# Weight gradient: narrow G of slice 0 alone in 1 KB rows, slice 1's G whole by the software queue, and a finer first rounding

## Chip, cores, metric

One core of one Trainium2 chip. Time is device microseconds of one launch; fast runs of the kernel before agree within 0.35 us in each set, so a change of less than 0.2 us is read from profiles, not from a few times. Instruction times count from the span's start; the span is about 1.8 us shorter than the time of the launch. A transfer has landed when its completion semaphore has its full count. TensorE starts at half clock: the trace records when it goes to full clock, and the spacing of 512-column matmuls shows it too (0.43 us apart before, 0.216 after).

## The reference

`grad_weight[k, n] = sum over b, m of input[b, m, k] * grad_output[b, m, n]`, with 16 x 512 rows, K = 1024, N = 768, all fp32. Called X and G below: the 8192 rows are 64 slices of 128.

## The kernel before

X and G are rounded to bf16 on their way. From slice 2 on, the software queue (GpSimd) casts while it loads. Slices 0 and 1 come mostly by the hardware queues of SyncE and ScalarE as fp32 and are rounded by VectorE (DVE) and ScalarE (ACT), so that TensorE (PE) can start early. Each slice needs 12 matmuls of 512 columns: eight "wide" ones (blocks A and B; G columns 0 to 511 against eight blocks of X), and four "narrow" ones (N; G columns 512 to 767, two turned blocks, against two halves of X). PE first runs warm-up matmuls on constants.

```python
ORDER = "A1! B1 N1 B2! N2 A2 N3! A3 B3 A4! ...".split()      # cut; "B2!" = block B up to slice 1, then close its banks
WARMUP = [512] * 10 + [128] * 2

xf = [head.tile([P, K], f32, name=f"xf{s}") for s in range(2)]
gf = head.tile([P, NA], f32, name="gf")                      # NA = 512
gnf = head.tile([P, 2, NB], f32, name="gnf")                 # NB = 256
nc.sync.dma_start(out=gf, in_=G[0:P, 0:NA])
nc.scalar.dma_start(out=xf[0], in_=X[0:P, :])
nc.sync.dma_start(out=gnf, in_=G[0 : 2 * P, NA:N].rearrange("(s p) n -> p s n", p=P))
nc.scalar.dma_start(out=xf[1], in_=X[P : 2 * P, :])
# ... warm-up matmuls
gwide[1] = head.tile([P, NA], bf16, name="g1")
nc.gpsimd.dma_start(out=gwide[1], in_=G[P : 2 * P, 0:NA])
for s in range(2, S):                                        # gt, then xt, of each slice on the software queue
    ...

def add_slice(part, i, s, first, last):                      # cut
    ...
    if part.first:
        copy_out(dst, bank, i)                               # even i on DVE, odd i on ScalarE
        if s == 0 and i == 0:
            round_narrow(0)                                  # DVE: narrow G of slice 0, behind the copy of bank 0
```

## Time and profile before

| | before |
|---|---|
| time, median (range) | 176.97 us (176.78 to 176.98; the 3 runs known at the prediction) |
| PE busy | 169.8 of 175.0 us, 97% |
| first real matmul | 5.37 us |
| first narrow matmul | 7.82 us, though PE could go on at 7.11 |
| block B of slice 1 | 8.84 us; from there on PE never waits |

PE's busy share alone says "nothing to gain". The chain of waits and the timeline of the first 9 us, shown in the prediction, say where some 0.9 us of avoidable waiting lies: at the head, before and among the first four narrow matmuls.

### The profile page before, as it was taken

To read this page: it belongs to the slowest core of one execution; us is meant where nothing else is said; L and a number is where in the kernel's file an instruction comes from. 1 tells how busy PE (TensorE), PEld (TensorE's weight loads), DVE (VectorE), ACT (ScalarE), POOL (GpSimd) and SP (SyncE) were. 2 spreads that over 40 slices of the span, in tenths; PEclk is the share of its full clock that TensorE was granted. 3 is DMA by queue.
4 is the path that set the end of the run, shared out by engine and by line. 5 is a ranking of instruction groups with operands and counts; after the bars stand their busy time and mean duration, and the time that the engine had idled before them with its cause. 6 is when DMAs were issued, how large, how long until landed. Compare 5 with 4: busy or idle time off the path is not lost.

```text
span 175.0 us, 2012 instructions
## 1 busy us (share of the span) xinstructions
PE 169.8 (97%) x793; PEld 78.2 (45%) x808; DVE 61.5 (35%) x103; ACT 6.3 (4%) x12; POOL 66.4 (38%) x129
## 2 busy tenths in 40 slices
PE   8799999999999999999999999999999999999993
PEld 3244444444444444444444444444444444444463
DVE  0665574791950029400000561300460003932122
ACT  2640000000000000000000000000000000000000
POOL 7444443444444444444444444444174200000000
PEclk9999999999999999999999999999999999999999
DMA  5999999999999999999999999999999990085623
GB/s 189 290 207 208 209 208 207 208 208 209 209 207 207 209 208 209 208 209 207 208 208 208 208 211 206 208 208 209 209 207 209 208 184 3 0 182 161 167 93 120
DMA packets 25176, 33.42 MB, mean 191 GB/s; under 512 B 6480, under 2 KB 16720, under 8 KB 25168
## 3 DMA queue, kind: packets, MB, share of 16 engines
q0 software_dynamic: 18000, 28.58, 89.3%
q1 hardware_dynamic: 2720, 2.62, 4.6%
q10 hardware_dynamic: 4448, 2.10, 4.6%
q8 instruction: 6, 0.10, 0.2%
q14 instruction: 2, 0.02, 0.0%
HBM read 58.72 MB, written 3.15 MB: 353 GB/s over the span
## 4 chain that ended last, share of the span: by engine, by line
PE 93%; DMA 4%; issue 1%; DVE 0%; SPq 0%
PE bank L126 62%; PE bank L133 32%; DMA gnf<-in_grad_output_dram 4%; SPq L74 0%; DVE gn L114 0%; DVE acc L117 0%
## 5 line engine op out<-in xcount | busy, mean ns | idle before, releaser
L126 PE MATMUL bank<-gt,xt 128*128 128x512 bf16 (+2 forms) x515 | 108.3, 367 | 0.5
L126 PEld LDWEIGHTS <-xt 128*128 128x128 bf16 x524 | 50.2, 98 | 57.3
L117 DVE TENSOR_TENSOR acc<-bank,acc 128x512 f32<-128x512 f32 (+2 forms) x62 | 37.9, 666 | 73.4 <-PE bank L126 73.0
L133 PE MATMUL bank<-xt,gt 128*128 128x512 bf16 x242 | 54.8, 379 | 0.3
L98 POOL DMA_DIRECT2D xt<-in_input_dram x62 | 32.9, 531 | 37.7 <-DMA xt<-in_input_dram 35.2
L97 POOL DMA_DIRECT2D gt<-in_grad_output_dram x62 | 32.9, 531 | 31.9 <-DMA gt<-in_grad_output_dram 28.0
L133 PEld LDWEIGHTS <-gt 128*128 128x128 bf16 x248 | 24.3, 98 | 29.3
L117 DVE TENSOR_TENSOR acct<-bank,acct 128x512 f32<-128x512 f32 x24 | 15.7, 682 | 30.0 <-PE bank L133 29.9
L83 PE MATMUL bank<-const-bfloat16-1.0 128*128 128x512 bf16 (+1 forms) x12 | 4.3, 534 | 0.8 <-PEq L263 0.8
L126 PE MATMUL bank<-g,x 128*128 128x512 bf16 x16 | 4.0, 380 | 0.3 <-DVE x L110 0.3
L83 PEld LDWEIGHTS <-const-bfloat16-1.0 128*128 128x128 bf16 x12 | 1.5, 135 | 3.3 <-issue 3.2
L179 DVE STREAM_TRANSPOSE turned<-acct 128x512 f32<-128x512 f32 x4 | 2.9, 714 | 0.1
L121 DVE COPY acc<-bank 128x512 f32<-128x512 f32 x4 | 2.7, 686 | 0.6 <-PE bank L126 0.6
L133 PE MATMUL bank<-x,gn 128*128 128x512 bf16 x8 | 2.2, 380 | 0.5 <-DVE gn L114 0.5
L126 PEld LDWEIGHTS <-x 128*128 128x128 bf16 x16 | 1.5, 97 | 2.2 <-DVE x L110 0.5
L123 ACT COPY acc<-bank 128x512 f32<-128x512 f32 x4 | 2.1, 589 | 1.8 <-PE bank L126 1.8
L110 DVE CAST g<-gf 128x256 bf16<-128x256 f32 x1 | 0.3, 295 | 4.7 <-DMA gf<-in_grad_output_dram 4.7
L121 DVE COPY acct<-bank 128x512 f32<-128x512 f32 x2 | 1.3, 684 | 1.3 <-PE bank L133 1.3
L133 PEld LDWEIGHTS <-gn 128*128 128x128 bf16 x8 | 0.7, 98 | 1.9 <-DVE gn L114 1.0
L111 ACT CAST x<-xf 128x256 bf16<-128x256 f32 x4 | 1.4, 402 | 0.2 <-DMA xf<-in_input_dram 0.2
L111 ACT ACT_TABLE_LOAD x1 | 1.3, 1283 | 1.7 <-PEq L263 1.7
L123 ACT COPY acct<-bank 128x512 f32<-128x512 f32 x2 | 1.1, 589 | 1.5 <-PE bank L133 1.5
(8 smaller groups left out, 3.0 us busy)
## 6 DMA issues: line engine op xcount, KB each, us to landing
xt<-in_input_dram POOLq DMA_DIRECT2D x62, 256.0 KB, 8.5
gt<-in_grad_output_dram POOLq DMA_DIRECT2D x62, 192.0 KB, 8.5
out_dram<-acc SPq DMA_DIRECT2D x13, 128.0 KB, 2.7
xf<-in_input_dram ACTq DMA_DIRECT2D x2, 512.0 KB, 5.2
out_dram<-turned ACTq DMA_DIRECT2D x4, 256.0 KB, 3.4
gf<-in_grad_output_dram SPq DMA_DIRECT2D x1, 256.0 KB, 3.9
gnf<-in_grad_output_dram SPq DMA_DIRECT2D x1, 256.0 KB, 6.3
out_dram<-acc SPq DMA_DIRECT2D x1, 256.0 KB, 2.0
```

The lines of the kernel that those rows point to most:

```text
L83: nc.tensor.matmul(wps[:, 0:cols], ones, nc.const_aps.tensor(1.0, (P, cols), bf16), start=True, stop=True,)
L97: nc.gpsimd.dma_start(out=gt, in_=G[s * P : (s + 1) * P, :])
L98: nc.gpsimd.dma_start(out=xt, in_=X[s * P : (s + 1) * P, :])
L110: nc.vector.tensor_copy(out=dst[:, c : c + QX], in_=src[:, c : c + QX])
L111: nc.scalar.copy(out=dst[:, c + QX : c + 2 * QX], in_=src[:, c + QX : c + 2 * QX])
L117: nc.vector.tensor_add(out=dst, in0=src, in1=dst)
L121: nc.vector.tensor_copy(out=dst, in_=src)
L123: nc.scalar.copy(out=dst, in_=src)
L126: nc.tensor.matmul(bank, xs[s][:, k * P : (k + 1) * P], gwide[s][:, c0:c1], start=start, stop=stop)
L133: nc.tensor.matmul(bank, gnarrow[s].rearrange("p (r t) -> p t r", t=NT)[:, t], xs[s][:, h * NA : (h + 1) * NA], start=start, stop=stop,)
L179: nc.vector.transpose(out=turned[:, h * hb : (h + 1) * hb, :, t], in_=dst.rearrange("p (b r) -> p b r", r=SQ),)
```

## The change

The intent: narrow G of slice 0 should not have to share its transfer with slice 1's narrow G, whose rows take turns with X of slice 1. Slice 1's G goes whole to the software queue, which casts it, so DVE's cast of slice 1's narrow G falls away. DVE's first cast of X is cut to 128 columns, so that the first matmul starts sooner.

```diff
-    gf = head.tile([P, NA], f32, name="gf")
-    gnf = head.tile([P, 2, NB], f32, name="gnf")
-    nc.sync.dma_start(out=gf, in_=G[0:P, 0:NA])
+    gf = head.tile([P, N], f32, name="gf")
+    nc.sync.dma_start(out=gf[:, 0:NA], in_=G[0:P, 0:NA])
     nc.scalar.dma_start(out=xf[0], in_=X[0:P, :])
-    nc.sync.dma_start(out=gnf, in_=G[0 : 2 * P, NA:N].rearrange("(s p) n -> p s n", p=P))
+    nc.sync.dma_start(out=gf[:, NA:N], in_=G[0:P, NA:N])
     nc.scalar.dma_start(out=xf[1], in_=X[P : 2 * P, :])
...
-    nc.gpsimd.dma_start(out=gwide[1], in_=G[P : 2 * P, 0:NA])
-    for s in range(2, S):
+    for s in range(1, S):
         gt = xg.tile([P, N], bf16, name="gt")
         nc.gpsimd.dma_start(out=gt, in_=G[s * P : (s + 1) * P, :])
...
+    round_by("DVE", g0, gf, 0, 256)
+    round_by("ACT", g0, gf, 256, NA)
+    round_by("DVE", xs[0], xf[0], 0, P)
+    round_by("ACT", xs[0], xf[0], 2 * P, 4 * P)
+    round_by("DVE", xs[0], xf[0], P, 2 * P)
+    round_by("DVE", xs[0], xf[0], 4 * P, 6 * P)
+    round_by("ACT", xs[0], xf[0], 6 * P, 8 * P)
...
             if s == 0 and i == 0:
-                round_narrow(0)
+                round_by("DVE", g0, gf, NA, N)
```

More of the change, by code (lines that the diff above doesn't have):

```diff
@@ L89, with round_by @@
         )
-    gwide[1] = head.tile([P, NA], bf16, name="g1")
-    nc.gpsimd.dma_start(out=gwide[1], in_=G[P : 2 * P, 0:NA])
-    for s in range(2, S):
+    for s in range(1, S):
         gt = xg.tile([P, N], bf16, name="gt")
-        xt = xg.tile([P, K], bf16, name="xt")
         nc.gpsimd.dma_start(out=gt, in_=G[s * P : (s + 1) * P, :])
-        nc.gpsimd.dma_start(out=xt, in_=X[s * P : (s + 1) * P, :])
-        xs[s] = xt
         gwide[s] = gt[:, 0:NA]
         gnarrow[s] = gt[:, NA:N]
-    QX = 256
-    gwide[0] = head.tile([P, NA], bf16, name="g0")
+        if s > 1:
+            xs[s] = xg.tile([P, K], bf16, name="xt")
+            nc.gpsimd.dma_start(out=xs[s], in_=X[s * P : (s + 1) * P, :])
     for s in range(2):
         xs[s] = head.tile([P, K], bf16, name=f"x{s}")
-        gnarrow[s] = head.tile([P, NB], bf16, name=f"gn{s}")
-    def round_pair(dst, src, c):
-        nc.vector.tensor_copy(out=dst[:, c : c + QX], in_=src[:, c : c + QX])
-        nc.scalar.copy(out=dst[:, c + QX : c + 2 * QX], in_=src[:, c + QX : c + 2 * QX])
-    def round_narrow(s):
-        nc.vector.tensor_copy(out=gnarrow[s], in_=gnf[:, s, :])
+    g0 = head.tile([P, N], bf16, name="g0")
+    gwide[0] = g0[:, 0:NA]
+    gnarrow[0] = g0[:, NA:N]
+    def round_by(engine, dst, src, c0, c1):
+        copy = nc.vector.tensor_copy if engine == "DVE" else nc.scalar.copy
+        copy(out=dst[:, c0:c1], in_=src[:, c0:c1])
+    round_by("DVE", g0, gf, 0, 256)
[5 more added lines that the diff above has]
+    round_by("ACT", xs[0], xf[0], 6 * P, 8 * P)
     def add_out(dst, src):
@@ L209, in bank_by_bank @@
                 add_slice(part, i, s, s == first, s == upto - 1)
-    round_pair(gwide[0], gf, 0)
-    round_pair(xs[0], xf[0], 0)
-    round_pair(xs[0], xf[0], NA)
     for i, step in enumerate(ORDER):
         if i == 2:
-            round_pair(xs[1], xf[1], NA)
-            round_pair(xs[1], xf[1], 0)
-            round_narrow(1)
+            round_by("DVE", xs[1], xf[1], 4 * P, 6 * P)
+            round_by("ACT", xs[1], xf[1], 6 * P, 8 * P)
+            round_by("DVE", xs[1], xf[1], 0, 2 * P)
+            round_by("ACT", xs[1], xf[1], 2 * P, 4 * P)
         close = step.endswith("!")
```

## The prediction

> **What bounds the kernel now.** I read the page's busy shares first, then the chain that ended last, then the same chain in order of time, then the timeline of the first 12 us, and at last the trace's records of single instructions, DMA packets and landings for that stretch.
>
> Page, busy shares and chain:
>
> ```profile
> PE 169.8 (97%) x793; PEld 78.2 (45%) x808; DVE 61.5 (35%) x103; ACT 6.3 (4%) x12; POOL 66.4 (38%) x129
> ...
> PE 93%; DMA 4%; issue 1%; DVE 0%; SPq 0%
> PE bank L126 62%; PE bank L133 32%; DMA gnf<-in_grad_output_dram 4%; SPq L74 0%; DVE gn L114 0%; DVE acc L117 0%
> ```
>
> The matmuls are the bound, and only one thing besides them is on the chain: the transfer of narrow G into gnf. In order of time (start us, us, what):
>
> ```profile
> 1.18 6.27 DMA gnf<-in_grad_output_dram
> 7.45 0.02 issue
> 7.47 0.30 DVE gn L114
> 7.77 0.05 issue
> 7.82 1.19 PE bank L133 x4
> 9.01 0.86 PE bank L126 x4
> 9.87 0.86 PE bank L133 x4
> ```
>
> From 7.82 us to the last matmul the chain never leaves PE except for 0.05 us pieces of issue. So the end can be moved only by moving the step at 7.8 us, and whatever is gained there is gained at the end, provided that no later wait appears. The timeline shows who waits around it:
>
> ```profile
> 5.37 1.90 PE L126 MATMUL bank<-g,x 128*128 128x512 bf16 x8 [0.33 <-DVE x L110]
> 5.80 0.69 DVE L121 COPY acc<-bank 128x512 f32<-128x512 f32 x1 [0.28 <-PE bank L126]
> ...
> 7.47 0.29 DVE L114 CAST gn<-gnf 128x256 bf16<-128x256 f32 x1 [0.98 <-DMA gnf<-in_grad_output_dram]
> 7.68 0.68 DVE L121 COPY acc<-bank 128x512 f32<-128x512 f32 x1
> ...
> 7.82 1.19 PE L133 MATMUL bank<-x,gn 128*128 128x512 bf16 x4 [0.55 <-DVE gn L114]
> ...
> 8.84 1.02 PE L126 MATMUL bank<-g,x 128*128 128x512 bf16 x4
> ```
>
> A steady matmul of 512 columns takes 0.216 us from start to start. The eighth matmul of slice 0's wide blocks starts at 6.89 and would let the next go at 7.11; the first narrow one starts at 7.82: **0.71 us lost**. The four narrow ones start at 7.82, 8.05, 8.41 and 8.63 and slice 1's block B follows at 8.84: 1.02 us where four need 0.86, so **0.16 us more lost**. That second loss is the same wait at one remove: the third narrow matmul writes the third bank, whose copy on DVE (7.68 to 8.36) stands in program order behind the rounding of narrow G, which sat waiting for the transfer. After 8.84 no matmul is late.
>
> **What the Trainium skill says.**
> "DMA: Bandwidth & Descriptors", Queues, rings and completion order: each of the 16 engines takes turns between the queues it has work for, packet by packet. The trace agrees: from 5.50 to 6.25 us 44 rows of 1 KB (SyncE's queue), 41 of 4 KB (ScalarE's) and 40 of the software queue ended. A 1 KB row costs a turn like a 4 KB one. The first 128 rows of gnf got through between 4.08 and 4.76, in the gap before X of slice 1 was flowing; the second 128 ran from 4.72 to 6.96, turn by turn.
> The same page, Anatomy of one DMA: most of a transfer's fixed cost is the receipt of the write. Here: G of slice 1's last packet ended at 7.22 and the transfer landed at 7.62, so 0.4 us; gnf 6.96 to 7.45, 0.5 us.
> "VectorE: DVE Perf Modes", Mode 2×_2P: a copy from SBUF can do two fp32 elements a cycle, one from PSUM can't. Trace: two casts of 256 columns in a row start 0.21 us apart, two bank copies of 512 columns 0.61 apart. It agrees (at the page's 0.96 GHz, 256/2 cycles are 0.13 us and 512 cycles 0.53, leaving 0.08 fixed in both).
> "TensorE: Matmul & The Clock Gate", Wait — 56ns, not 53.3ns?: 215.7 ns between warm matmuls of 512 columns; the trace shows 0.216.
>
> **The change, part by part.**
> *Narrow G of slice 0 alone on SyncE's queue.* 256 rows of 1 KB become 128. The first 128 of before ended at 4.76; with 0.5 us of receipt I put the landing at about **5.3 us instead of 7.45**. Then it is no longer what anyone waits for. The rounding of narrow G stands on DVE behind the copy of bank 0, as before. That copy starts at about 5.73 (0.07 earlier, below), the next DVE instruction 0.60 later: rounding from 6.33 to 6.62, so the narrow matmuls may start at 6.67, before PE is through with its eight (7.03). Copy of bank 2: 6.54 to 7.22; the third narrow matmul wants it at 7.46. Both losses vanish: 0.71 + 0.16 = **0.87 us**.
>
> *Finer rounding.* The built programs show DVE with two casts of 128 columns and one of 256 where it had two of 256; ScalarE keeps its three of 256 columns. The first matmul waits in before for the cast that ran from 5.017 to 5.311 and starts at 5.368. X of slice 0 landed at 4.99, so the start can't go below that; ScalarE's half of G is ready at 5.08. By the 2-per-cycle rate a cast of 128 columns is 128/2/0.96 = 0.067 us shorter: **0.07 us** gained, an estimate. The second cast, 0.15 us later, ends at about 5.39, in time for the second matmul at 5.52. One extra instruction on DVE (0.08 us fixed) hits nothing, as DVE is idle before the first bank copy. This 0.07 counts only because the narrow wait is gone.
>
> *Slice 1's G whole by the software queue.* One transfer of 128 rows of 3 KB (1.5 KB as bf16) in place of 2 KB (1 KB). A software packet of 1.5 KB takes 135 ns, of 1 KB 96 ns: 8 rows an engine x 39 ns = 0.31 us more. Against it 8 rows an engine of 1 KB x 46 ns = 0.37 us less on SyncE's queue. The engines are busy throughout, so all that follows in the software queue moves by about -0.06 us: nothing. X of slice 1, with one rival fewer, should land at or a little before 7.27. G of slice 1 must land after all else of the head has had its turn: about 7.5 to 7.7, as now (7.62). Block B of slice 1 wants it at 5.30 + 12 x 0.216 = **7.90**. Margin 0.2 to 0.4 us: thin. Its X must be rounded by then too: DVE is free at about 7.14, X lands at 7.0 to 7.27, a cast takes 0.29: ready at 7.6.
>
> *Later.* With PE 0.94 us earlier, does a slice come too late? X of slices 2, 3, 4, 6, 8 landed at 9.73, 11.93, 14.14, 18.55 and 22.95; their first use was at 11.43, 14.05, 15.8, 20.1 and 25.3. The smallest margin is 1.5 us, over 0.5 after the change. At the end of the stream the last X landed at 145.2 and the narrow pass reaches it at about 147. No new wait.
>
> Sum: 0.71 + 0.16 + 0.07 = 0.94 us, 0.5% of 176.97. **176.97 - 0.94 = 176.03, say 176.05 us.**
>
> **The rivals.**
> *G of slice 1 becomes the new wait.* It now carries both the wide and the narrow part and still starts late (its first packet ran at 5.20, though issued at 1.23). For it: margin of 0.2 to 0.4 us, and rows half as long again. Against: the byte budget ahead of it shrank by as much. If it lands at 8.2, block B starts at 8.25 and 0.35 of the gain is lost: 176.4. If at 8.8, nothing is left: 176.9.
> *The transfer was not the cause, only the last of several.* The rounding of X of slice 1 (ScalarE waited for its landing until 7.29) also stands near. If X of slice 1 lands no earlier and DVE gets to it late, block B starts near 7.9 anyway; that rival costs 0.1 at most, 176.15.
> *The single tile for wide and narrow G makes the first rounding wait for both transfers.* I looked at the waits of the built program: the first roundings wait for the first transfer alone and the narrow one for the second. Ruled out; it would have cost some 0.3 us.
> *Software stream later.* If longer first rows delayed all slices by 0.3 us, margins of 0.5 still hold; no change.
>
> **Range and chances.** Before repeated within 0.2 us (176.78 to 176.98). Full gain 176.05, about three in four; a part of it lost to slice 1's G, one in five, up to 176.5; a somewhat larger gain from an earlier X, to 175.75. Range 175.75 to 176.5. A change of 2% would be 3.5 us, and all idle time of PE after its warm-up is 1.2 us, so faster than 2% is out of reach; slower would need a stall nobody shows.
>
> **What will show it.** Right: gf's narrow part lands near 5.3; DVE rounds it at about 6.3 right behind the first bank copy; first X matmul at 5.30; narrow matmuls from 7.03 without a gap; slice 1's block B at about 7.90, against 8.84; chain without the narrow transfer, with X of slice 0 or wide G of slice 0 at its head. Wrong: PE idle before slice 1's block B with the wait put down to gt or X of slice 1, or an idle gap of PE between 9 and 30 us.

## The result

**176.02 us** median (175.84 to 176.60, 4 runs), before 176.89 us (4 runs): ratio 0.9957, interval 0.9933 to 0.9981. Ratios here are the mean time of one kernel's fast runs over that of the other's in the same rounds, so not quite the ratio of the medians quoted. The gain is 0.0043 x 176.89 = 0.76 us.

The page of the changed kernel, busy shares and chain:

```profile
PE 169.9 (97%) x793; PEld 78.4 (45%) x808; DVE 61.3 (35%) x103; ACT 6.2 (4%) x12; POOL 66.7 (38%) x129
...
PE 97%; issue 0%; DVE 0%
PE bank L127 63%; PE bank L134 32%; PE bank L81 3%; DVE acc L118 0%
```

No transfer is on the chain any more. Its head is now the warm-up matmuls (L81): in this execution the profile gives PE no wait from its first instruction to its last (but PE's weight load waited 0.17 us for the first cast of X, so the first real matmul still hangs on X of slice 0, landed at 5.02). PE's busy time is the same 169.9 us; what went is idle time. The timeline of the head (start us, us, engine, line, operation, what it waited for):

```profile
5.32 1.55 PEld L127 LDWEIGHTS <-x 128*128 128x128 bf16 x8 [0.17 <-DVE x L107]
5.32 2.04 PE L127 MATMUL bank<-g,x 128*128 128x512 bf16 x8
5.89 0.69 DVE L122 COPY acc<-bank 128x512 f32<-128x512 f32 x1 [0.28 <-PE bank L127]
...
6.50 0.28 DVE L107 CAST g<-gf 128x256 bf16<-128x256 f32 x1
6.70 0.68 DVE L122 COPY acc<-bank 128x512 f32<-128x512 f32 x1
...
7.20 1.03 PE L134 MATMUL bank<-x,g 128*128 128x512 bf16 x4
...
8.06 1.03 PE L127 MATMUL bank<-gt,x 128*128 128x512 bf16 x4
```

The cast of narrow G at 6.50 stands right behind the first bank copy with no wait in brackets: the data was there (it landed at 5.84). Four narrow matmuls run from 7.20 to 8.06 without the gap. Block B of slice 1 starts 0.78 us earlier than before (8.06 for 8.84); the last matmul starts 0.78 us earlier too (171.25 for 172.03), and the span ends 0.77 us earlier.

One thing is new. The first eight matmuls took 2.04 us where the same eight took 1.90 before. The single records show the second following the first after 0.36 us instead of 0.23: the trace records TensorE's switch to full clock at 5.63 us in this execution, and at 4.50 in that of before.

### The profile page after: what moved, and what is told of

Its sections match the earlier page's. It is cut to its first block, busy times and chain, and to the rows that moved or that the text cites. A ratio compares the mean times of both kernels' runs of the same rounds, so it can differ in the third digit from the quotient of the medians.

```text
span 174.3 us, 2013 instructions
## 1 busy us (share of the span) xinstructions
PE 169.9 (97%) x793; PEld 78.4 (45%) x808; DVE 61.3 (35%) x103; ACT 6.2 (4%) x12; POOL 66.7 (38%) x129
## 4 chain that ended last, share of the span: by engine, by line
PE 97%; issue 0%; DVE 0%
PE bank L127 63%; PE bank L134 32%; PE bank L81 3%; DVE acc L118 0%
## 5 line engine op out<-in xcount | busy, mean ns | idle before, releaser
L92 POOL DMA_DIRECT2D gt<-in_grad_output_dram x63 | 33.8, 536 | 31.2 <-DMA gt<-in_grad_output_dram 24.9
L81 PE MATMUL bank<-const-bfloat16-1.0 128*128 128x512 bf16 (+1 forms) x12 | 4.6, 574 | 0.8 <-PEq L263 0.8
L81 PEld LDWEIGHTS <-const-bfloat16-1.0 128*128 128x128 bf16 x12 | 1.6, 140 | 3.5 <-issue 3.5
L127 PE MATMUL bank<-gt,x 128*128 128x512 bf16 x8 | 2.1, 379 | 0.0
L127 PE MATMUL bank<-g,x 128*128 128x512 bf16 x8 | 2.0, 398 | 0.0
L107 DVE CAST x<-xf 128x256 bf16<-128x256 f32 (+1 forms) x5 | 1.0, 260 | 0.0
```

Source lines behind the costliest of these rows:

```text
L81: nc.tensor.matmul(wps[:, 0:cols], ones, nc.const_aps.tensor(1.0, (P, cols), bf16), start=True, stop=True,)
L92: nc.gpsimd.dma_start(out=gt, in_=G[s * P : (s + 1) * P, :])
L107: copy(out=dst[:, c0:c1], in_=src[:, c0:c1])
L127: nc.tensor.matmul(bank, xs[s][:, k * P : (k + 1) * P], gwide[s][:, c0:c1], start=start, stop=stop)
```

## The experiments

Each kernel ran 5 rounds (5 runs; 6 of round_late and head2) beside the kernel before on the same chip (median 176.82 to 176.88 us there).

| run | what | median us | ratio to before (interval) | block B of slice 1 at |
|---|---|---|---|---|
| again | the changed kernel | 176.04 | 0.9951 (0.9938 to 0.9963) | 7.84 |
| coarse | without the finer cast | 176.02 | 0.9958 (0.9945 to 0.9970) | 8.24 |
| old_transfers | finer cast only | 176.77 | 0.9998 (0.9984 to 1.0011) | 8.78 |
| split_only | narrow transfer cut in two only | 176.59 | 0.9985 (0.9972 to 0.9997) | 8.04 |
| split_mended | the same, one store fewer | 176.49 | 0.9966 (0.9953 to 0.9979) | 8.48 |
| split_mended2 | repeated | 176.22 | 0.9965 (0.9952 to 0.9979) | 8.13 |
| tail_more | changed, one store more | 176.47 | 0.9980 (0.9968 to 0.9992) | 7.94 |
| g1_late | changed, slice 1's G later | 176.52 | 0.9980 (0.9967 to 0.9993) | 8.58 |
| round_late | before, cast behind bank 2 | 176.67 | 1.0000 (0.9980 to 1.0020) | 8.78 |
| round_late2 | repeated | 176.83 | 0.9998 (0.9986 to 1.0011) | 8.67 |
| head | changed, X of slice 0 in halves | 177.17 | 1.0020 (1.0008 to 1.0032) | 8.87 |
| head2 | changed, a quarter of X on SyncE | 177.72 | 1.0064 (1.0030 to 1.0097) | 10.10 |

### again: the changed kernel, once more

> The changed kernel unaltered, for a tighter interval and a second look at the head. Theory (the narrow transfer was the whole wait, block B of slice 1 starts as soon as PE is through): 0.8 to 0.95 us under the kernel before, 175.95 to 176.1. In the first profile the TensorE clock reached full speed only at 5.63 us and the first real matmul ran cold; in the profile of before it did at 4.50. If that switch moves from run to run, this kernel, which no longer waits at 7.1 us, scatters more than the one before, by up to some 0.5 us upwards. Rival: the scatter of the first measurement (175.84 to 176.6) was chance and this one repeats within 0.2 us.

The gain is 0.0049 x 176.86 = 0.87 us. Its profile fell on an early clock switch (4.30 us) and shows the head as it was predicted; the chain in order of time first, then the timeline:

```profile
0.74 4.19 DMA xf<-in_input_dram
5.24 1.90 PE bank L127 x8
7.14 0.86 PE bank L134 x4
```

```profile
5.24 1.90 PE L127 MATMUL bank<-g,x 128*128 128x512 bf16 x8 [0.30 <-DVE x L107]
...
6.28 0.28 DVE L107 CAST g<-gf 128x256 bf16<-128x256 f32 x1
...
6.98 1.03 PE L134 MATMUL bank<-x,g 128*128 128x512 bf16 x4
...
7.84 1.03 PE L127 MATMUL bank<-gt,x 128*128 128x512 bf16 x4
```

With the clock up in time the chain's head is X of slice 0, landed at 4.93. Block B of slice 1 starts 1.00 us before its old place and the last matmul starts 0.93 us before (171.10). The 0.07 us between the two went at 30.3 us, where PE's weight load waits for X of slice 11 (slices counted by the program's order of matmuls):

```profile
30.35 0.55 PEld L127 LDWEIGHTS <-xt 128*128 128x128 bf16 x4 [0.39 <-DMA xt<-in_input_dram]
```

The matmul before it started at 30.07, so this one could have gone at 30.28; it started at 30.35. It is a new wait, small, and the next limit of this kernel. The five runs lie between 175.82 and 176.23: 0.41 us, more than the 0.2 of the rival and within the 0.5 of the theory.

### coarse: without the finer cast

```diff
-    round_by("DVE", xs[0], xf[0], 0, P)
+    round_by("DVE", xs[0], xf[0], 0, 2 * P)
-    round_by("DVE", xs[0], xf[0], P, 2 * P)
```

> The changed kernel with one cast of 256 columns on DVE in place of the two of 128. Theory: the first real matmul starts 0.07 us later and everything after it too: 0.05 to 0.1 us slower than the changed kernel, 176.05 to 176.15; below what five rounds can prove, but the profile shows the start at 5.37 to 5.40 instead of 5.32. Rival (the finer rounding carries the gain): 176.8, the time of before.

```profile
5.37 2.18 PE L126 MATMUL bank<-g,x 128*128 128x512 bf16 x8
8.24 1.03 PE L126 MATMUL bank<-gt,x 128*128 128x512 bf16 x4
```

The first real matmul started at 5.37, 0.13 us later than in again; X of slice 0 had landed 0.06 later, which leaves 0.07 for the cast. All profiles with X of slice 0 in one transfer bear it out: from its landing to the first real matmul it is 0.31 us in the five with the finer cast (the changed kernel, again, old_transfers, tail_more, g1_late) and 0.37 to 0.38 in the seven without. The time can't show it: the median is that of the changed kernel, and the intervals overlap. Here the profile decides, and only for the start: what stood in the way next was the clock (full at about 5.97 us, from the spacing of the matmuls), so block B of slice 1 came at 8.24.

### old_transfers: the finer cast alone

```diff
-    round_pair(xs[0], xf[0], 0)
+    nc.vector.tensor_copy(out=xs[0][:, 0:P], in_=xf[0][:, 0:P])
+    nc.scalar.copy(out=xs[0][:, 2 * P : 4 * P], in_=xf[0][:, 2 * P : 4 * P])
+    nc.vector.tensor_copy(out=xs[0][:, P : 2 * P], in_=xf[0][:, P : 2 * P])
```

> The kernel before with only the finer rounding of slice 0: both narrow parts still come in one transfer on SyncE's queue, wide G of slice 1 by the software queue. Theory: the narrow matmuls wait for that transfer until about 7.8 us whatever the start, so 0.00 us gained: 176.85 to 177.0. Rival (finer rounding helps by itself): 176.8 or less by 0.07; first rival in its strong form (it carries the gain): 176.0.

Nothing gained, as the theory said; the interval, 0.24 us to either side, would not exclude the 0.07 of the weaker rival, so the profile is what speaks. Timeline of its head:

```profile
5.21 1.90 PE L126 MATMUL bank<-g,x 128*128 128x512 bf16 x8 [0.62 <-DVE x L212]
...
7.41 0.29 DVE L114 CAST gn<-gnf 128x256 bf16<-128x256 f32 x1 [1.08 <-DMA gnf<-in_grad_output_dram]
...
7.76 1.19 PE L133 MATMUL bank<-x,gn 128*128 128x512 bf16 x4 [0.65 <-DVE gn L114]
```

PE starts 0.16 us earlier than in the kernel before and waits 0.10 us longer at the narrow matmuls: the narrow transfer (landed 7.38) sets the time, whatever the start.

### split_only: the narrow transfer cut in two, nothing moved to the software queue

```diff
-    nc.sync.dma_start(out=gnf, in_=G[0 : 2 * P, NA:N].rearrange("(s p) n -> p s n", p=P))
+    for s in range(2):
+        nc.sync.dma_start(out=gnf[:, s, :], in_=G[s * P : (s + 1) * P, NA:N])
```

> The kernel before with the narrow transfer cut in two on the same queue, slice 0's 128 rows first; nothing moves to the software queue, rounding as before. Theory (what matters is only that slice 0's rows no longer wait for slice 1's): slice 0's narrow part lands at 5.3 to 5.9, block B of slice 1 starts at about 7.95, gain about 0.85: 176.0 to 176.15. Rival (the move of slice 1's narrow part off SyncE's queue is needed too, as it competes with X of slice 1): X of slice 1 lands at 7.27 as before, block B of slice 1 starts at 8.1 or later, 176.3 or more.

The theory missed the time, but not the head: block B of slice 1 started at 8.04, 0.80 us earlier than before. The rival's "176.3 or more" holds, but not for its reason: X of slice 1 landed at 7.08, not 7.27. The last matmul started 0.69 us earlier (171.34; the missing 0.11 is again the wait for X of slice 11, landed at 30.54), and the end came only 0.27 us earlier. So 0.42 us went after the last matmul: from its start to the end of the span 3.44 us, in the kernel before 3.02. The waits of SyncE's queue in the last 6 us, first before, then split_only (us in total, times, longest):

```profile
SPq L274 <- DMA out_dram<-acc: 0.7, 1, 0.7
```

```profile
SPq L275 <- DMA out_dram<-acc: 1.1, 1, 1.1
```

The single records tell why. At the end SyncE waits for the transfers' semaphores in a list of nine waits, 0.06 us each, eight of them for two semaphores at once. The hardware queues' transfers take eight of these semaphores in turn. In the kernel before the last store's comes in the ninth wait, at the end of that list, and the others have been ticked off while it was under way (1.6 us from its issue to the end of the list). One transfer more, and the last store's comes in the second wait: seven more follow after it.

### split_mended, split_mended2: the same with one store fewer

```diff
-            W = NB if k < 6 else c1 - c0
+            W = NB if k < 5 else c1 - c0        # block 5 in one store instead of two
```

> split_only with one store fewer at the end (the two stores of block 5 as one), so that it again has as many hardware-queue transfers as the kernel before. In split_only block B of slice 1 started at 8.04 us, 0.80 earlier than before, and the last matmul 0.69 earlier, but the end came only 0.26 earlier: from the last matmul to the end 3.44 us instead of 3.02. Theory (the 16 completion semaphores are waited for one by one at the end, 0.06 us each; one transfer more turned the last store's semaphore from the last waited for into the second, so that the rest of the list came after it): tail back at 3.0 us, total 176.0 to 176.2, as the changed kernel. Rival (slice 1's narrow part on SyncE's queue costs something further on): 176.5 to 176.6 as in split_only.

> split_mended once more, unaltered. Its five runs lay in two heaps, 176.01 and 176.16 against 176.49 to 176.52, and its profile (176.49) shows the clock's switch after five real matmuls, about 6.4 us, with block B of slice 1 at 8.48; the tail was 3.03 us as it should be. Theory (the split alone brings the gain, and a late clock switch costs up to 0.5 us of it by chance): runs between 175.9 and 176.6 again; in a profile with the switch before 5.3 us block B of slice 1 starts at 7.9 to 8.05. Rival (slice 1's narrow part on SyncE's queue costs something itself): all runs at 176.4 to 176.6 whatever the switch, or block B of slice 1 late with an early switch.

The wait at the end is back at 0.7 us and the tail at 3.02 to 3.03 us, in both. The runs of split_mended fall in two heaps, 176.01 and 176.16, and three at about 176.5. Its profile is of the second kind:

```profile
5.34 2.43 PE L127 MATMUL bank<-g,x 128*128 128x512 bf16 x8
7.61 1.03 PE L134 MATMUL bank<-x,gn 128*128 128x512 bf16 x4
8.48 0.81 PE L127 MATMUL bank<-g,x 128*128 128x512 bf16 x3
```

PE waits nowhere. The same eight matmuls took 2.43 us instead of 1.90, and the single records show why: the first ones start 0.40 to 0.43 us apart, which is half the rate, until about 6.46 us. So block B of slice 1 came at 8.48 by the clock, not by a transfer. In split_mended2's profile the switch came at 5.60 and block B of slice 1 at 8.13, after a late landing of X of slice 0 (5.13). So it is not the profile with an early switch that its theory asked for; split_only's is one (switch at 3.54, block B of slice 1 at 8.04, as forecast). Over the two, the split gains about 0.6 us; the changed kernel gained 0.87 in again and 0.76 in its first measurement. How the rest divides between the finer cast (0.07), later landings of X of slice 0 (4.97 to 5.13 in the three profiles with the split, 4.93 to 5.04 in those of the changed kernel, again and tail_more) and clock switches isn't settled; the intervals overlap.

### tail_more: one store more in the changed kernel

```diff
-            W = NB if k < 6 else c1 - c0
+            W = NB if k < 7 else c1 - c0        # block 6 in two stores instead of one
```

> The changed kernel with one store more: the wide part of block 6 in two stores of 256 columns instead of one of 512. Theory of the waits at the end (as for split_mended): tail 3.0 to 3.45 us, total 0.4 us over the changed kernel, 176.45, with the head unchanged. Rival (the number of transfers does not matter, the store itself is well hidden): 176.0.

The head is that of the changed kernel (block B of slice 1 at 7.94), the tail is 3.43 us, the median 176.47, 0.43 us over again. One transfer more costs this by itself.

### g1_late: slice 1's G second in the software queue

```diff
+    load_g(2)
+    load_g(1)
```

> The changed kernel with G of slice 1 issued second in the software queue, behind G of slice 2. Theory (G of slice 1 now has 0.4 to 0.6 us to spare and a wait in the head passes to the end one to one): it lands at about 8.46, block B of slice 1 starts at about 8.5 instead of 7.9 to 8.06, 0.4 to 0.6 us slower than the changed kernel: 176.4 to 176.6. Rival (later slack takes it up): 176.0. Rival (software queue slower at its start than I think): 176.9 or more.

The timeline of its matmuls:

```profile
6.97 1.03 PE L140 MATMUL bank<-x,g 128*128 128x512 bf16 x4
8.58 0.81 PE L133 MATMUL bank<-gt,x 128*128 128x512 bf16 x3 [0.58 <-DMA gt<-in_grad_output_dram]
```

G of slice 1 landed at 8.54 and block B of slice 1 started at 8.58, 0.52 us later than in the first profile of the changed kernel; the last matmul started 0.52 us later too, and the median rose by 0.5 us. A wait in the head goes to the end in full (from block B of slice 1 to the last matmul both took 163.18 us), and the slack of slice 1's G in the changed kernel is smaller than the 1.05 us it was delayed here.

### round_late, round_late2: the narrow cast behind the copy of bank 2, in the kernel before

```diff
-            if s == 0 and i == 0:
+            if s == 0 and i == 2:
```

> The kernel before, with DVE's rounding of narrow G of slice 0 put behind the copy of bank 2 instead of ahead of it. Theory (the 0.16 us gap inside the four narrow matmuls is that copy, held up in DVE's order behind a cast that waits for its transfer): narrow matmuls still start at 7.8, but without the gap; block B of slice 1 at 8.68 instead of 8.84, 0.15 us faster than before: 176.75. Rival (the gap is something else): gap stays, 176.9.

> round_late once more, unaltered, as one run of 177.87 us widened its interval to 0.998 to 1.002. Theory: the gap inside the narrow matmuls stays away (four in 0.87 us), and the time lies 0.1 to 0.15 us under the kernel before, ratio 0.9990 to 0.9995. Rival (the gap is only moved): same as before, ratio 1.0000, with a gap between the narrow matmuls and block B of slice 1.

Timeline of round_late2:

```profile
7.80 1.04 PE L133 MATMUL bank<-x,gn 128*128 128x512 bf16 x4 [0.63 <-DVE gn L114]
...
8.67 0.59 PE L126 MATMUL bank<-g,x 128*128 128x512 bf16 x2
```

The gap inside the four narrow matmuls is gone in both profiles (0.87 us from the first to block B of slice 1, 1.02 before), so it was the bank copy held up behind the cast. That this is worth 0.15 us is not shown by the times: the ratio is 1.0000 and 0.9998 in the two sets (one run of 177.87 us weighs on the first).

### head and head2: can X of slice 0 come sooner?

```diff
-    nc.scalar.dma_start(out=xf[0], in_=X[0:P, :])
+    for c in (0, NA):                                   # head; and 8 warm-ups of 512, one of 128
+        nc.scalar.dma_start(out=xf[0][:, c : c + NA], in_=X[0:P, c : c + NA])
```

> The changed kernel, going on from it: X of slice 0 comes in two transfers of 512 columns, so that the first half and wide G of slice 0 land together at about 3.8 us; two and a half warm-up matmuls fewer. Theory (the head is now bound by the landing of X of slice 0 at 5.0): first real matmul at about 4.35, then block B of slice 1 is bound by landing of G and X of slice 1 (7.0 to 7.5) and starts at about 7.5 instead of 8.06: 0.4 to 0.55 us faster than the changed kernel, 175.5. Rival (the first matmuls only run in the cold clock, at half the rate, and the start is given back): 175.9 to 176.0. Rival (shorter rows slow X of slice 0's second half): 176.0 or more.

The start did move, to 4.85 us, but block B of slice 1 went the other way, to 8.87, behind X of slice 1. In the list of transfers and their times to landing, X of slice 1 stands as:

```profile
xf<-in_input_dram ACTq DMA_DIRECT2D x1, 512.0 KB, 6.8
```

It was issued at 1.67 us, its first packet ran at 5.37 and it landed at 8.49; in the changed kernel it was issued at 1.18, ran from 4.33 and landed at 7.03. It had become the third transfer of its queue. This kernel also has one transfer too many for the tail (3.44 us).

```diff
+    nc.scalar.dma_start(out=xf[0][:, 0 : 6 * P], in_=X[0:P, 0 : 6 * P])     # head2, in place of the whole xf[0];
+    nc.sync.dma_start(out=xf[0][:, 6 * P : K], in_=X[0:P, 6 * P : K])       # one store fewer at the end
```

> The changed kernel with the last quarter of X of slice 0 moved from ScalarE's to SyncE's queue ahead of narrow G, and one store fewer at the end to keep the number of transfers. Theory (the changed kernel's first matmul is held by the landing of X of slice 0 at 4.93 to 5.02, which has twice the bytes of wide G on its queue): three quarters land at about 4.65, first real matmul at 4.95 to 5.05, block B of slice 1 at about 7.6 if G of slice 1 (7.42 to 7.49) and X of slice 1 allow it: 0.2 to 0.3 us faster than the changed kernel, 175.75. Rival (in a run whose clock switches late the earlier matmuls only run cold): 175.9 to 176.05. Rival (the extra transfer delays X of slice 1 as in the kernel called head, where it landed at 8.49): over 176.3.

Worse still. Three quarters of X landed at 4.73, but narrow G, now third on SyncE's queue, ran its first packet at 5.60 and held the narrow matmuls to 9.08. In its profiled run (179.76, the slowest of six) the trace records the clock at half rate again from 10.23 to 13.64 us, after a wait of 2.0 us before the narrow matmuls; no other profile has it before the last microsecond. In all five profiles with three transfers on a queue (head, head2 and the three of the split) the third's first packet ran between 5.37 and 5.60 us, though issued at about 1.65. That is from 0.02 us before to 0.24 us after the start of the second transfer's last packet on the same queue (completion writes counted), so the third stood behind the second; whether that order is the whole reason, no run tests. Neither of the two kernels that put X of slice 0 into two transfers gained by it, and no experiment beat the changed kernel.

## Why the prediction was right

**The bound and the place of the gain.** Right: old_transfers, which keeps the narrow transfer, gains nothing; the kernels that free slice 0's narrow G from slice 1's start block B of slice 1 earlier, and the last matmul moves with it, but for head and head2, in which a third transfer on a queue is the new wait.

**The sum, 0.71 + 0.16 + 0.07 = 0.94 us.** Again has both gaps at 0 and the first matmul 0.13 us earlier, of which 0.07 is the cast and 0.06 an earlier landing of X, which is luck: block B of slice 1 is 1.00 us earlier. Then 0.07 is lost at 30.3 us, so its last matmul is 0.93 us earlier, its time 0.87. That 0.93 meets 0.94 so closely is two unforeseen things that cancel. In the first profile the two gaps were 0 as well, but 0.14 us came back as a first matmul at half clock: 0.78. Measured by time: 0.76 and 0.87.

**Narrow G lands at 5.3.** Too early by half a microsecond: 5.84, in again 5.73. The last of its 128 rows ended at 5.27 and 5.19, not at 4.76 as the first 128 of the longer transfer had; why is not settled (the trace doesn't say which of those 256 rows were slice 0's, and X of slice 1, which the forecast had flow only after the first 128, ran from 4.43). From the last row to the landing it took 0.57 and 0.54 us, near the forecast's 0.5. The passage of the Trainium skill that the forecast names for the receipt ("DMA: Bandwidth & Descriptors", Anatomy of one DMA) is written for the software queue's path and makes it most of about 2 us; the traces here have 0.4 us there and 0.5 to 0.6 on SyncE's queue, and they decide. The late landing cost nothing, as DVE comes to it only at 6.50 and 6.28. Here the margin carried the forecast, not the figure.

**The rival, slice 1's G as the new wait.** It landed at 7.49 and 7.42, a little ahead of the stated 7.5 to 7.7, and block B of slice 1 never waited for it. G1_late shows the price had it been late.

**"Later. No new wait."** Wrong, by 0.07 us. The forecast looked at X of slices 2, 3, 4, 6 and 8 and took 1.5 us as the smallest margin. In the same profile X of slice 11 landed at 30.36 and its first matmul started at 31.29: 0.93 us, no more than the forecast gain. In the changed kernel's first profile, with the late clock, 0.35 us of it was left; in again nothing was, and PE waited. In split_only and split_mended2 it waited too, for 0.11 and 0.08 us. So the head has little left to give while X of slice 11 lands where it does (30.1 to 30.6 us in all runs but head): by these margins, not by a run, head could not have reached its 175.5, whatever its start.

**Not foreseen: the clock.** The forecast put all matmuls at 0.216 us from 5.30 on. In the kernel before, a late switch to full clock would hide in the wait at 7.1 us (argued: no profile of it has one); with the wait gone it shows. In seven profiles block B of slice 1 waits for no transfer. From the first real matmul to block B of slice 1, twelve matmuls, it took 2.60 us where the switch came before them (again, tail_more, split_only), and 2.63, 2.74, 2.88 and 3.14 with the switch at 5.60, 5.63, about 5.97 and about 6.46 (split_mended2, the first profile of the changed kernel, coarse, split_mended). The first measurement's 176.60 is not explained by it. Its granted clock is 0.998, not 1.0; in the profiles that have this figure the half rate comes at the very end, 170.67 us after a switch at 3.5 to 3.6 us, so by that pattern its switch was early too, and its cause is open.

## What to carry to other kernels

Where PE is 97% busy, the head is the place to look: follow the chain to its last step that isn't PE, and count a landing by the rows that stand ahead of and beside it on the 16 engines, not by its own bytes. List the margin of every later transfer, not of the first few: the one that a gain at the head meets next was the slice 11 that the forecast had left out. Then check what the removed wait had been hiding, and, after any change in the number of transfers, compare the time from the last matmul to the end: here one transfer more cost half of the whole change, and one store fewer took it back.

## What the Trainium skill lacked or had wrong

- "TensorE: Matmul & The Clock Gate", What's actually happening: it has the switch to full clock vary by ±500 ns with the phase of a free-running window, though it also says that one kernel showed 6, 11 or 14 slow matmuls, by the phase at its start. In the 14 profiles here, all with the first warm-up matmul at 0.78 us, it came between 3.40 us and about 6.46 us, a spread of 3.1 us.
- "DMA: Bandwidth & Descriptors", Specifications: first byte after about 1 us by the software queue and 0.6 by the hardware queues. Here G of slice 1, issued at 1.23 us, had its first packet at 5.20 us in the profile of before, with seven more transfers issued behind it by then; wide G of slice 0, issued at 0.74, at 1.76 us.
- No page I read has a figure for how long a transfer stands behind others on its queue: the third on one hardware queue, issued at about 1.65 us, ran its first packet at 5.37 to 5.60 us in five of five profiles, close behind the last packet of the second; the second, issued at 1.18, ran from 3.6 to 4.6.
- No page I read has it: the end of the program waits for the transfers' semaphores one by one, 0.06 us each in a fixed order; where the last store's comes early in the list, the end is 0.4 us later (3.43 to 3.44 us after the last matmul's start instead of 3.01 to 3.03).
